# Feed-forward layers by seven block products instead of eight

## The chip, the cores and the metric

The kernel runs on one core of one Trainium2 chip. The metric is the device time of one execution in microseconds (us). The core has five engines, each with its own queue of instructions worked off in order: PE (TensorE, matrix products into PSUM), DVE (VectorE, elementwise), ACT (ScalarE, elementwise and functions), POOL (GpSimd, elementwise, reaches SBUF alone) and SP (which issues most DMAs). Semaphores make one engine wait for another.

## The reference

Two encoder layers are applied to 544 tokens (512 of a prompt, 32 of a sample) of 1024 features. Each layer is a feed-forward half step, a mixer (pooling, short convolution, differential attention with one input and one output projection) and a second feed-forward half step, each closed by a layer norm:

```python
def swiglu(x, w_in, w_out):
    gate, up = jnp.split(x @ w_in, 2, axis=-1)
    return (jax.nn.silu(gate) * up) @ w_out
...
    x = layer_norm(ALPHA * x + 0.5 * swiglu(x, w_ffn_in[0], w_ffn_out[0]), ln_g[0], ln_b[0])
    proj = x @ w_in
...
    x = layer_norm(ALPHA * x + mix, ln_g[1], ln_b[1])
    x = layer_norm(ALPHA * x + 0.5 * swiglu(x, w_ffn_in[1], w_ffn_out[1]), ln_g[2], ln_b[2])
```

The feed-forward width is 2816 (22 tiles of 128), so `w_in` is 1024 x 5632 and `w_out` 2816 x 1024. There are four such half steps, called FFNs here. Everything is float32.

## The kernel before

Activations lie feature by token: a tile is 128 features x 544 tokens, and all of x is eight tiles (`y[k]`). A product is taken on 128 features of output and half of the tokens (272) at a time, in one PSUM bank of six (`bank()`). To keep float32 accuracy each operand is split in a high and a low part that PE takes at one pass each: ACT copies the rounded high part (`whi`, `xh`, `hh`), DVE subtracts it from the original to give the low part (`wlo`, `xl`, `hl`). Each 128 x 128 block of weights then takes three matmuls on 272 columns: high by high, low by high (`mm_h`, L199), high by low (`mm_l`, L204).

Weights come from HBM by SP's queue into `raw` buffers, 512 KB at a time. `Weights.group` (L159 on ACT, L160 on DVE) splits 128 x 512 pieces into eight pairs of buffers. `W.get()` hands out the next tile and loads up to two tiles ahead.

`ffn` takes the 22 tiles of inner features in three parts, `FSPLIT = (8, 7, 7)`. In a part each inner tile needs a gate tile and an up tile: 8 blocks of weights x 3 matmuls x 2 halves x 2 = 96 matmuls. ACT takes the SiLU of the gate (L448), DVE multiplies by up (L449), and the result is split into `hh` and `hl` (L232, L233). Then eight output tiles are taken over the part's inner tiles and added to `y` (`resid`, L343 and L345). The last part ends in `out_phase`, where layer-norm sums run beside the products: DVE subtracts a shift from each finished tile, ACT squares it, POOL adds to two accumulators (L267 to L271, `acc1`, `acc2`). The last two output tiles (four in the very last layer norm) stand at the end by halves, so that the layer norm of the first half of the tokens runs beside the second half's products. `start` then takes the first two tiles of the next product while the layer norm is applied tile by tile.

The order on each engine is not that of the code: a scheduler that builds the program lays instructions out by readiness and priority, and semaphores keep what depends on what.

## Time and profile before

| | |
|---|---|
| time, median of 3 runs | 2105.5 us (2105.45 to 2107.89) |
| time of the profiled execution | 2106.86 us |
| span of the profiled execution, first to last instruction | 2104.7 us |
| PE busy | 2079.3 us, 99% of the span, 16286 matmuls |
| DVE busy | 1013.1 us, 48% |
| ACT busy | 771.6 us, 37% |
| POOL busy | 228.8 us, 11% |
| chain that ended last | PE 95%, DVE 2% |

The time is that of the whole execution; the span is what the trace shows of it and is 2.2 us shorter. Busy time counts a stretch once, also where two instructions of an engine overlap. A busy PE is not PE at its peak, since matmuls overlap in the records: how many matmuls start in a stretch says more than the mean length of one.

### The profile page before, as it was taken

How to read it: one execution, taken by the hardware profiler on the slowest of the kernel's cores; microseconds unless marked ns; L12 is line 12 of the kernel's file. 1: busy time of each engine (PE TensorE's matmuls, PEld its weight loads, DVE VectorE, ACT ScalarE, POOL GpSimd, SP SyncE). 2: the span in 40 equal slices, each digit the busy share in tenths (PEclk: the TensorE clock that was granted, in tenths of full speed). 3: DMA queues.
4: the chain of work that ended last, by engine and by line, in shares of the span. 5: the costliest groups of instructions: out<-in, count | busy, mean ns of one | idle time of the engine just before them, and what ended most of it. 6: DMA issues, size and time to landing. Idle time of an engine off the chain costs nothing.

```text
span 2104.7 us, 38545 instructions
## 1 busy us (share of the span) xinstructions
PE 2079.3 (99%) x16286; PEld 2042.2 (97%) x16286; DVE 1013.1 (48%) x1970; ACT 771.6 (37%) x1591; POOL 228.8 (11%) x216
## 2 busy tenths in 40 slices
PE   9999999999999999999999999999999999999997
PEld 9999999999999999999999999999999999999997
DVE  4333333776556333333653333347766553333337
ACT  5323223565435323223443232235653353222233
POOL 0000000511133000000420000006011320000003
PEclk9999999999999999999999999999999999999999
DMA  7322222132232222222232222222321222222221
GB/s 240 99 91 83 90 91 84 59 115 92 62 119 81 91 86 86 84 98 82 70 101 83 89 88 89 89 85 67 109 93 54 78 91 82 90 89 82 91 83 61
DMA packets 61749, 189.13 MB, mean 90 GB/s; under 512 B 8932, under 2 KB 13156, under 8 KB 61576
## 3 DMA queue, kind: packets, MB, share of 16 engines
q1 hardware_dynamic: 52592, 173.18, 25.9%
q10 hardware_dynamic: 8984, 13.49, 2.0%
q8 instruction: 128, 2.10, 0.4%
q14 instruction: 45, 0.37, 0.1%
HBM read 179.88 MB, written 8.34 MB: 89 GB/s over the span
## 4 chain that ended last, share of the span: by engine, by line
PE 95%; DVE 2%; POOL 1%; ACT 1%; issue 1%; DMA 0%; SPq 0%; POOLq 0%; ACTq 0%
PE b L199 59%; PE b L204 30%; PE b L629 1%; PE b L628 1%; PE o L644 1%; POOL xl L333 1%; PE b L609 0%; ACT ya L327 0%; DVE z L322 0%; PE b L716 0%; POOL rstd L302 0%; PE b L682 0%; DVE diag L308 0%; DVE acc L286 0%; PE b L311 0%
## 5 line engine op out<-in xcount | busy, mean ns | idle before, releaser
L199 PE MATMUL b<-xh,whi 128*128 128x272 f32 x3456 | 1000.0, 291 | 6.2 <-ACT xh L332 3.7
L199 PE MATMUL b<-xh,wlo 128*128 128x272 f32 x3456 | 993.5, 289 | 0.3 <-DVE wlo L160 0.3
L204 PE MATMUL b<-xl,whi 128*128 128x272 f32 x3456 | 978.2, 288 | 0.2
L160 DVE TENSOR_TENSOR wlo<-raw,whi 128x512 fp32r<-128x512 f32 (+1 forms) x656 | 469.7, 719 | 694.8 <-ACT whi L159 692.7
L159 ACT ACTIVATE whi<-raw 128x512 fp32r<-128x512 f32 (+1 forms) x656 | 403.3, 619 | 858.7 <-PE b L204 569.8
L199 PEld LDWEIGHTS b<-xh,whi 128*128 128x128 f32 x3456 | 651.7, 189 | 9.5 <-ACT xh L332 5.9
L199 PEld LDWEIGHTS b<-xh,wlo 128*128 128x128 f32 x3456 | 653.1, 189 | 1.5 <-DVE wlo L160 0.8
L204 PEld LDWEIGHTS b<-xl,whi 128*128 128x128 f32 x3456 | 644.6, 188 | 2.1 <-POOL xl L333 1.5
L199 PE MATMUL b<-hh,wlo 128*128 128x272 f32 x1408 | 406.2, 289 | 0.0
L199 PE MATMUL b<-hh,whi 128*128 128x272 f32 x1408 | 405.2, 288 | 0.0
L204 PE MATMUL b<-hl,whi 128*128 128x272 f32 x1408 | 404.6, 287 | 0.0
L199 PEld LDWEIGHTS b<-hh,wlo 128*128 128x128 f32 x1408 | 264.9, 188 | 0.2
L204 PEld LDWEIGHTS b<-hl,whi 128*128 128x128 f32 x1408 | 264.9, 188 | 0.2
L199 PEld LDWEIGHTS b<-hh,whi 128*128 128x128 f32 x1408 | 264.9, 188 | 0.0
L278 POOL TENSOR_TENSOR ya<-ya,shift 128x544 f32<-128x544 f32 x14 | 24.8, 1792 | 1412.9 <-DVE wlo L160 1386.4
L448 ACT ACTIVATE sg<-b 128x272 f32<-128x272 f32 x176 | 69.6, 397 | 213.1 <-PE b L204 213.0
L449 DVE SCALAR_TENSOR_TENSOR sg<-b,sg 128x272 f32<-128x272 f32 x176 | 77.6, 441 | 130.9 <-PE b L204 119.2
L343 DVE SCALAR_TENSOR_TENSOR ya<-ya,b 128x272 f32<-128x272 f32 x88 | 38.5, 438 | 88.7 <-PE b L204 87.8
L333 POOL TENSOR_TENSOR xl<-ya,xh 128x272 fp32r<-128x272 f32 x80 | 70.3, 901 | 30.8 <-ACT xh L332 25.1
L345 DVE TENSOR_TENSOR ya<-ya,b 128x272 f32<-128x272 f32 x108 | 46.7, 433 | 54.0 <-PE b L204 53.8
L232 ACT ACTIVATE hh<-sg 128x544 fp32r<-128x544 f32 (+1 forms) x100 | 59.1, 591 | 32.6 <-DVE sg L449 32.5
L233 DVE TENSOR_TENSOR hl<-sg,hh 128x544 fp32r<-128x544 f32 (+1 forms) x100 | 65.2, 652 | 7.2 <-ACT hh L232 7.1
(183 smaller groups left out, 1455.9 us busy)
## 6 DMA issues: line engine op xcount, KB each, us to landing
raw<-in_w SPq DMA_DIRECT2D x206, 512.0 KB, 3.5
raw<-in_w SPq DMA_DIRECT2D x64, 448.0 KB, 3.3
raw<-in_wi SPq DMA_DIRECT2D x40, 512.0 KB, 3.5
raw<-in_wo SPq DMA_DIRECT2D x16, 512.0 KB, 3.5
U<-scr ACTq DMA_DIRECT2D x8, 320.0 KB, 4.8
out_nkT<-k ACTq DMA_DIRECT2D x8, 272.0 KB, 2.1
out_nvT<-vT ACTq DMA_DIRECT2D x8, 272.0 KB, 2.1
out_yT<-ya SPq DMA_DIRECT2D x16, 136.0 KB, 1.8
```

The source lines that it names most:

```text
L159: S.activation(out=hi[:, :e], in_=raw[:, g:g + e], func=AF.Copy)
L160: V.tensor_tensor(out=lo[:, :e], in0=raw[:, g:g + e], in1=hi[:, :e].bitcast(F32), op=ALU.subtract)
L199: PE.matmul(acc[:, :HALF], v[:, cs], x[k][0][:, HS[h]], start=first and i == 0, stop=False)
L204: PE.matmul(acc[:, :HALF], w[k // 4][0][:, cs], x[k][1][:, HS[h]], start=False, stop=last)
L232: S.activation(out=hh[:, sl], in_=t[:, sl], func=AF.Copy)
L233: (eng or V).tensor_tensor(out=hl[:, sl], in0=t[:, sl], in1=hh[:, sl].bitcast(F32), op=ALU.subtract)
L278: POOL.tensor_tensor(out=c, in0=c, in1=self.s, op=ALU.subtract)
L333: POOL.tensor_tensor(out=xl[:, sl], in0=c, in1=xh[:, sl].bitcast(F32), op=ALU.subtract)
L343: V.scalar_tensor_tensor(out=c, in0=c, scalar=ALPHA, in1=a, op0=ALU.mult, op1=ALU.add)
L345: V.tensor_tensor(out=c, in0=c, in1=a, op=ALU.add)
L448: S.activation(out=sg[:, sl], in_=g[:, :HALF], func=AF.Silu)
L449: V.scalar_tensor_tensor(out=sg[:, sl], in0=u[:, :HALF], scalar=0.5, in1=sg[:, sl], op0=ALU.mult, op1=ALU.mult)
```

## The change

A product of a 2 x 2 arrangement of weight blocks with a 2 x 2 arrangement of activation blocks is eight block products; with sums of blocks formed beforehand, seven are enough. Here one dimension is the two halves of the tokens, one the two of a pair of input tiles (or input halves), and one the two outputs: gate and up of an inner tile, or two output tiles. `Weights.sums` forms four sums of weight blocks on DVE (L212 of the changed kernel) and splits seven groups (L177 on ACT, L178 on DVE) where four were split before. `Blocks.add` forms four sums of activations (L318 to L321) and splits two further tiles, `s56` and `s73`: on DVE for the x of each FFN, on POOL for pairs of inner tiles. `seven` takes the seven products (L343), called here by 0 to 6, into three banks in the order a, b, a, c, a, c, a; a bank is read after each product (`after`) and the next product of the same bank adds to what stands there, so it waits for that reading.

In each FFN the first two inner tiles (`NPLAIN`) are taken as before, the other 20 by `hidden`, with seven products of 12 matmuls. Output tiles are taken in pairs over parts of 4, 6, 6 and 6 inner tiles, by seven products of 6 or 9 matmuls, and added to `y` by `resid7` (L573, L575) after each product. The first part's outputs stand after the fifth inner tile, the second's after the eleventh, the third's after the seventeenth. In the last part the first pair and the last pair (the last two in the last layer norm) are taken as before. `W.get` loads one unit ahead; a unit is all seven groups. The tiles of the sums and of the layer norm lie in a pool `xb` that gives way to the mixer's pool. The weights are laid out by blocks on the host; their bytes are the same.

```diff
-FSPLIT = (8, 7, 7)
+FSPLIT = (4, 6, 6, 6)
+NPLAIN = 2
-RAW_BUFS = 2
+RAW_BUFS = 3
+XB = 23
...
+        def sums(self, b11, b12, b22, b21):
+            n = b11.shape[-1]
+            def add(a, b):
+                r = wp.tile([P, G], F32, tag="sum", name="sum", bufs=3)[:, :n]
+                V.tensor_tensor(out=r, in0=a, in1=b, op=ALU.add)
+                return r
+            g11, g21 = self.group(b11), self.group(b21)
+            r1 = add(b11, b12)
+            r2 = add(r1, b22)
+            g2, g1 = self.group(r2), self.group(r1)
+            g3 = self.group(add(b12, b22))
+            g22 = self.group(b22)
+            return g11, g21, g2, g1, g3, g22, self.group(add(r2, b21))
...
+        def add(self, e, o, eng, new):
+            h0, h1 = HS
+            t1, t2 = tmp("s56"), tmp("s73")
+            eng.tensor_tensor(out=t1[:, h0], in0=e[:, h1], in1=o[:, h1], op=ALU.subtract)
+            eng.tensor_tensor(out=t1[:, h1], in0=t1[:, h0], in1=e[:, h0], op=ALU.subtract)
+            eng.tensor_tensor(out=t2[:, h0], in0=e[:, h0], in1=e[:, h1], op=ALU.subtract)
+            eng.tensor_tensor(out=t2[:, h1], in0=o[:, h0], in1=t1[:, h1], op=ALU.add)
+            s = [f(n) for f, n in zip(new, ("s56", "s73"))]
+            split(t1, s[0])
+            split(t2, s[1])
+            self.sums.append(s)
+        def products(self):
+            e, o = ([self.plain[p[i]] for p in self.pairs] for i in range(2))
+            s56, s73 = ([s[i] for s in self.sums] for i in range(2))
+            for xs, h in ((e, 0), (o, 0), (s56, 1), (s56, 0), (s73, 0), (s73, 1), (o, 1)):
+                yield [tuple(v[:, HS[h]] for v in x) for x in xs]
+    def seven(ws, blocks, after):
+        banks = {}
+        for i, (w, xs, name) in enumerate(zip(ws, blocks.products(), "abacaca")):
+            opens = name not in banks
+            acc = banks.setdefault(name, bank() if opens else None)
+            for j, (xh, xl) in enumerate(xs):
+                cs = slice(j * P, (j + 1) * P)
+                for m, (v, x) in enumerate(((w[0], xh), (w[1], xh), (w[0], xl))):
+                    PE.matmul(acc[:, :HALF], v[:, cs], x, start=opens and j == 0 and m == 0,
+                              stop=j == len(xs) - 1 and m == 2, skip_group_check=True)
+            after[i](acc[:, :HALF])
...
+            if blocks and m:
+                seven(W.get(), blocks, resid7(m, alpha))
+                for i in range(2):
+                    done(m + i)
+                m += 2
+                continue
...
+    def resid7(m, alpha):
+        seen = set()
+        def step(i, h, op):
+            def f(acc):
+                c = y[m + i][:, HS[h]]
+                if alpha and (i, h) not in seen:
+                    V.scalar_tensor_tensor(out=c, in0=c, scalar=ALPHA, in1=acc, op0=ALU.mult, op1=op)
+                else:
+                    V.tensor_tensor(out=c, in0=c, in1=acc, op=op)
+                seen.add((i, h))
+            return f
+        add, sub = ALU.add, ALU.subtract
+        return [step(0, 0, add), step(0, 0, add), step(1, 0, sub), step(1, 1, add), step(1, 1, sub), step(1, 0, add),
+                step(0, 1, add)]
+    def hidden(ws, blocks):
+        sg = tmp("sg")
+        up = tp.tile([P, HALF], F32, tag="up", name="up", bufs=2)
+        h0, h1 = HS
+        copy = lambda out: lambda acc: S.activation(out=out, in_=acc, func=AF.Copy)
+        def times(u, sl):
+            V.scalar_tensor_tensor(out=sg[:, sl], in0=u, scalar=0.5, in1=sg[:, sl], op0=ALU.mult, op1=ALU.mult)
+        def c12(acc):
+            V.tensor_tensor(out=sg[:, h0], in0=acc, in1=sg[:, h0], op=ALU.subtract)
+            S.activation(out=sg, in_=sg, func=AF.Silu)
+            times(up, h0)
+        seven(ws, blocks, [
+            copy(up),
+            lambda acc: V.tensor_tensor(out=up, in0=acc, in1=up, op=ALU.add),
+            copy(sg[:, h0]),
+            copy(sg[:, h1]),
+            lambda acc: V.tensor_tensor(out=sg[:, h1], in0=sg[:, h1], in1=acc, op=ALU.subtract),
+            c12,
+            lambda acc: times(acc, h1),
+        ])
+        return sg
+    def is_last(l, f):
+        return l == DEPTH - 1 and f == 1
+    def plan(final):
+        ends = [sum(FSPLIT[:s + 1]) for s in range(len(FSPLIT))]
+        for i in range(NF):
+            yield 1, i, "p" if i < NPLAIN else "s"
+            if i in ends:
+                yield from ((2, ends.index(i), p, "s") for p in range(NK // 2))
+        tail = 2 if final else 1
+        for p in range(NK // 2):
+            yield 2, len(FSPLIT) - 1, p, "p" if p == 0 or p >= NK // 2 - tail else "s"
     def ffn(l, f, x, pre):
-        for s, n in enumerate(FSPLIT):
-            hs = []
-            for i in range(n):
-                if pre:
-                    ga, ua = pre
-                    pre = None
+        xb = Blocks(x, [(k, k + NK // 2) for k in range(NK // 2)])
+        for k in range(NK // 2):
+            xb.add(y[k], y[k + NK // 2], V, (new_b, new_b))
+        sgs, parts = [], []
+        for what, i, *more in plan(is_last(l, f)):
+            if what == 1:
+                if i < NPLAIN:
+                    ua, ga = pre if i == 0 else [run(mm2(w, x, range(NK))) for w in W.get()]
+                    sg = tmp("sg")
+                    for sl, g, u in zip(HS, ga, ua):
+                        S.activation(out=sg[:, sl], in_=g[:, :HALF], func=AF.Silu)
+                        V.scalar_tensor_tensor(out=sg[:, sl], in0=u[:, :HALF], scalar=0.5, in1=sg[:, sl],
+                                               op0=ALU.mult, op1=ALU.mult)
                 else:
-                    ga = run(mm2(W.get(), x, range(NK)))
-                    ua = run(mm2(W.get(), x, range(NK)))
-                sg = tmp("sg")
-                hx = new_x("h")
-                for sl, g, u in zip(HS, ga, ua):
-                    S.activation(out=sg[:, sl], in_=g[:, :HALF], func=AF.Silu)
-                    V.scalar_tensor_tensor(out=sg[:, sl], in0=u[:, :HALF], scalar=0.5, in1=sg[:, sl],
-                                           op0=ALU.mult, op1=ALU.mult)
-                    if i == n - 1:
-                        split(sg, hx, sl)
-                if i < n - 1:
-                    split(sg, hx)
-                hs.append(hx)
-            if s < len(FSPLIT) - 1:
-                for m in range(NK):
-                    acc = run(mm2(W.get(), hs, range(n)))
-                    for h in range(2):
-                        resid(m, acc[h], h, s == 0)
+                    sg = hidden(W.get(), xb)
+                sgs.append(sg)
+                if len(sgs) < 2:
+                    continue
+                n = len(parts[-1].plain) if parts else 0
+                if not parts or n == FSPLIT[len(parts) - 1]:
+                    parts.append(Blocks([], []))
+                    n = 0
+                part = parts[-1]
+                for t in sgs:
+                    part.plain.append(new_x("h"))
+                    split(t, part.plain[-1])
+                part.pairs.append((n, n + 1))
+                part.add(*sgs, POOL, {0: (new_b, new_b), 2: (new_b, new_x)}.get(n, (new_x, new_x)))
+                sgs = []
+            elif i < len(FSPLIT) - 1:
+                seven(W.get(), parts[i], resid7(2 * more[0], i == 0))
             else:
-                return out_phase(l, 2 * f, hs, range(n), False)
+                part = parts[i]
+                return out_phase(l, 2 * f, part.plain, range(FSPLIT[i]), False, part)
```

**DVE in the middle of a part.** In the kernel before, one inner tile's rows on DVE are four splits of weights (L160), two multiplications (L449) and a split of the result (L233):

```order
L449 SCALAR_TENSOR_TENSOR sg<-b,sg 128x272
L160 TENSOR_TENSOR wlo<-raw,whi 128x512
L449 SCALAR_TENSOR_TENSOR sg<-b,sg 128x272
L160 TENSOR_TENSOR wlo<-raw,whi 128x512
L233 TENSOR_TENSOR hl<-sg,hh 128x544
L160 TENSOR_TENSOR wlo<-raw,whi 128x512 x2
```

In the changed kernel twelve rows from about one inner tile's stretch read so (L604, L595, L601, L592 read PSUM or make the gated product; L212 sums weights, L178 splits them, L291 splits activations):

```order
L604 TENSOR_TENSOR sg<-sg,b 128x272
L595 TENSOR_TENSOR sg<-b,sg 128x272
L178 TENSOR_TENSOR wlo<-raw,whi 128x512
L178 TENSOR_TENSOR wlo<-sum,whi 128x512
L592 SCALAR_TENSOR_TENSOR sg<-up,sg 128x272
L592 SCALAR_TENSOR_TENSOR sg<-b,sg 128x272
L212 TENSOR_TENSOR sum<-raw 128x512
L178 TENSOR_TENSOR wlo<-raw,whi 128x512
L291 TENSOR_TENSOR hl<-sg,hh 128x544
L178 TENSOR_TENSOR wlo<-raw,whi 128x512
L601 TENSOR_TENSOR up<-b,up 128x272
L178 TENSOR_TENSOR wlo<-sum,whi 128x512 x2
```

Four weight rows for one inner tile have become eleven, and two that take results have become five.

**DVE where output tiles are added.** Before, an addition to `ya` (L345) stands once for each half of an output tile, with a split of weights between:

```order
L345 TENSOR_TENSOR ya<-ya,b 128x272
L160 TENSOR_TENSOR wlo<-raw,whi 128x512
L345 TENSOR_TENSOR ya<-ya,b 128x272
L160 TENSOR_TENSOR wlo<-raw,whi 128x384
L345 TENSOR_TENSOR ya<-ya,b 128x272
L160 TENSOR_TENSOR wlo<-raw,whi 128x512
L345 TENSOR_TENSOR ya<-ya,b 128x272
```

After, in the third part's first pair of output tiles, additions (L575) stand one for one with splits and sums:

```order
L592 SCALAR_TENSOR_TENSOR sg<-b,sg 128x272
L178 TENSOR_TENSOR wlo<-raw,whi 128x384
L575 TENSOR_TENSOR ya<-ya,b 128x272
L178 TENSOR_TENSOR wlo<-raw,whi 128x384
L575 TENSOR_TENSOR ya<-ya,b 128x272
L178 TENSOR_TENSOR wlo<-sum,whi 128x384
L575 TENSOR_TENSOR ya<-ya,b 128x272
L178 TENSOR_TENSOR wlo<-sum,whi 128x384
L212 TENSOR_TENSOR sum<-sum,raw 128x384
L575 TENSOR_TENSOR ya<-ya,b 128x272
L178 TENSOR_TENSOR wlo<-sum,whi 128x384
```

An addition now follows every nine matmuls, and more of DVE's rows stand between two additions.

**PE in the second pair of output tiles of the second part.** With buffer numbers; `b_2428` is bank b, `b_2417` bank a, `b_2449` bank c; the rows are the end of product 1, two thirds of product 3, and the beginning of product 2:

```order
L343 MATMUL b_2428<-hl_2109,whi_2272 128x272
L343 MATMUL b_2449<-s56h_1522,whi_2284 128x272
L343 MATMUL b_2449<-s56h_1522,wlo_2285 128x272
L343 MATMUL b_2449<-s56l_1523,whi_2284 128x272
L343 MATMUL b_2449<-s56h_1820,whi_2284 128x272
L343 MATMUL b_2449<-s56h_1820,wlo_2285 128x272
L343 MATMUL b_2449<-s56l_1821,whi_2284 128x272
L343 MATMUL b_2417<-s56h_1522,whi_2280 128x272
L343 MATMUL b_2417<-s56h_1522,wlo_2281 128x272
```

Product 3 has been moved ahead of product 2 there. Product 2 adds to bank a, which DVE reads after product 0; product 3 opens a bank of its own.

## Rows read from the trace of the kernel before

**Rows 1.** The page: span, then busy time, share and instructions of engines.

```profile
span 2104.7 us, 38545 instructions
...
PE 2079.3 (99%) x16286; PEld 2042.2 (97%) x16286; DVE 1013.1 (48%) x1970; ACT 771.6 (37%) x1591; POOL 228.8 (11%) x216
```

**Rows 2.** The page: shares of the chain that ended last, by engine.

```profile
PE 95%; DVE 2%; POOL 1%; ACT 1%; issue 1%; DMA 0%; SPq 0%; POOLq 0%; ACTq 0%
```

**Rows 3.** PE by line and shape: instructions, busy us, mean ns, idle before.

```profile
L199 PE MATMUL b<-xh,whi 128*128 128x272 f32 x3456 | 1000.0, 291 | 6.2 <-ACT xh L332 3.7 <-ACT msq L299 1.6 <-ACT whi L159 0.7
...
L199 PE MATMUL b<-hh,whi 128*128 128x272 f32 x1408 | 405.2, 288 | 0.0
```

**Rows 4.** Windows: busy us and count of PE, weight loads, DVE, ACT, POOL; granted clock.

```profile
240.00:330.00 90.00, 90.00 (x723) 90.00 (x722) 33.89 (x60) 24.72 (x44) 0.00 (x0) 1.00 0.29 92
405.00:418.00 13.00, 10.80 (x82) 9.72 (x81) 11.56 (x31) 10.36 (x26) 7.65 (x11) 1.00 0.00 0
545.65:555.88 10.23, 10.23 (x39) 9.04 (x40) 3.85 (x10) 3.00 (x9) 0.00 (x0) 0.50 0.09 33
```

**Rows 5.** DVE by line and shape: count, busy us, mean ns, idle before.

```profile
L160 DVE TENSOR_TENSOR wlo<-raw,whi 128x512 fp32r<-128x512 f32 x592 | 427.5, 726 | 677.1 <-ACT whi L159 675.0
...
L233 DVE TENSOR_TENSOR hl<-sg,hh 128x544 fp32r<-128x544 f32 x76 | 54.7, 720 | 1.2 <-ACT hh L232 1.1
L345 DVE TENSOR_TENSOR ya<-ya,b 128x272 f32<-128x272 f32 x108 | 46.7, 433 | 54.0 <-PE b L204 53.8
```

**Rows 6.** Timeline of DVE, 26 to 29 us: start, us, instruction, count merged.

```profile
26.31 0.72 DVE L233 TENSOR_TENSOR hl<-sg,hh 128x544 fp32r<-128x544 f32 x1 [0.39 <-ACT hh L232]
26.95 1.89 DVE L160 TENSOR_TENSOR wlo<-raw,whi 128x512 fp32r<-128x512 f32 x3
...
28.85 0.68 DVE L160 TENSOR_TENSOR wlo<-raw,whi 128x512 fp32r<-128x512 f32 x1
```

**Rows 7.** Timeline of DVE, 405 to 418 us.

```profile
409.81 1.47 DVE L322 TENSOR_TENSOR z<-ya,b 128x272 f32<-128x272 f32 x4
...
411.21 0.42 DVE L316 TENSOR_TENSOR ya<-ya,o 128x272 f32<-128x272 f32 x1
```

**Rows 8.** Timelines of DVE and of POOL, 384 to 400 us.

```profile
384.49 1.82 POOL L271 TENSOR_TENSOR acc<-acc,sq 128x544 f32<-128x544 f32 x1
...
385.00 0.42 DVE L345 TENSOR_TENSOR ya<-ya,b 128x272 f32<-128x272 f32 x1
385.35 1.37 DVE L160 TENSOR_TENSOR wlo<-raw,whi 128x384 fp32r<-128x384 f32 x1
...
388.82 1.37 POOL L271 TENSOR_TENSOR acc<-acc,sq 128x544 f32<-128x544 f32 x1
...
389.48 1.25 DVE L160 TENSOR_TENSOR wlo<-raw,whi 128x512 fp32r<-128x512 f32 x1 [1.77 <-ACT whi L159]
...
398.42 1.36 POOL L271 TENSOR_TENSOR acc<-acc,sq 128x544 f32<-128x544 f32 x1
...
398.49 1.60 DVE L285 TENSOR_TENSOR acc<-acc,ya 128x272 f32<-128x272 f32 x1 [0.22 <-POOL acc L270]
```

**Rows 9.** POOL by line and shape.

```profile
L333 POOL TENSOR_TENSOR xl<-ya,xh 128x272 fp32r<-128x272 f32 x80 | 70.3, 901 | 30.8 <-ACT xh L332 25.1 <-ACT msq L299 4.6
L271 POOL TENSOR_TENSOR acc<-acc,sq 128x544 f32<-128x544 f32 x28 | 41.7, 1490 | 0.0
```

**Rows 10.** ACT by line and shape.

```profile
L159 ACT ACTIVATE whi<-raw 128x512 fp32r<-128x512 f32 x592 | 369.9, 630 | 829.3 <-PE b L204 540.4 <-issue 265.2 <-DMA raw<-in_w 15.7
L448 ACT ACTIVATE sg<-b 128x272 f32<-128x272 f32 x176 | 69.6, 397 | 213.1 <-PE b L204 213.0
...
L232 ACT ACTIVATE hh<-sg 128x544 fp32r<-128x544 f32 x76 | 48.9, 643 | 0.8 <-DVE sg L449 0.7
```

More of the change, by code (lines that the diff above doesn't have):

```diff
@@ new lines, in load @@
+        def load(self):
+            kind, src, n, step = self.units[self.loaded]
+            self.loaded += 1
+            if kind == "t":
+                raw = self.fetch()
+                nc.sync.dma_start(out=raw[:, :n], in_=src)
+                out = Tile([self.group(raw[:, g:min(g + G, n)]) for g in range(0, n, G)])
+            elif kind == "p":
+                out = self.pair([self.group(b) for b in self.blocks(src, n)], step)
+            else:
+                out = self.sums(*self.blocks(src, n))
+            self.ready.append(out)
@@ L188, in ahead, with get @@
                 self.load()
[L190 removed]
+        def get(self, n=None):
+            if n is None:
+                n = 2 if self.units[self.used][0] == "t" else 1
             self.used += 1
@@ L193, in get, with two @@
             return self.ready.pop(0)
+        def two(self):
+            return self.get(0) if self.units[self.used][0] == "p" else [self.get(0), self.get(0)]
     def mm_h(acc, w, x, k, h, first):
-        cs = slice((k % 4) * P, (k % 4) * P + P)
-        for i, v in enumerate(w[k // 4]):
-            PE.matmul(acc[:, :HALF], v[:, cs], x[k][0][:, HS[h]], start=first and i == 0, stop=False)
+        for i, v in enumerate(w.at(k)):
+            PE.matmul(acc[:, :HALF], v, x[k][0][:, HS[h]], start=first and i == 0, stop=False)
     def mm_l(acc, w, x, k, h, last):
-        cs = slice((k % 4) * P, (k % 4) * P + P)
-        PE.matmul(acc[:, :HALF], w[k // 4][0][:, cs], x[k][1][:, HS[h]], start=False, stop=last)
+        PE.matmul(acc[:, :HALF], w.at(k)[0], x[k][1][:, HS[h]], start=False, stop=last)
     def mm(acc, w, x, ks, h):
@@ L352, in out_phase, with done @@
         first = NK - nb
-        for m in range(first):
-            acc = run(mm2(W.get(), x, ks))
-            for h in range(2):
-                resid(m, acc[h], h, alpha)
+        tail = []
+        def done(m):
             if m == 1:
@@ L363, in out_phase, with tiles @@
                     ln.before(i, alpha)
-        tail = [W.get() for _ in range(nb)]
+        def tiles():
+            ws = W.get()
+            return ws if isinstance(ws, list) else [ws]
+        m = 0
+        while m < first:
+            if blocks and m:
+                seven(W.get(), blocks, resid7(m, alpha))
+                for i in range(2):
+                    done(m + i)
+                m += 2
+                continue
+            for w in tiles():
+                acc = run(mm2(w, x, ks))
+                for h in range(2):
+                    resid(m, acc[h], h, alpha)
+                done(m)
+                m += 1
+        while len(tail) < nb:
+            tail += tiles()
         def tail_mm(i, h):
```

129 lines of the change are left out of this document (80 added, 49 removed).

## The prediction

> **What bounds the kernel now.** I read the page's busy times first: PE is busy for 2079.3 of 2104.7 us, DVE for less than half [rows 1]. The chain that ended last says the same, 95% PE [rows 2]. A busy PE could still be slow, so the windows come next: in the middle of an FFN 723 matmuls start in 90.00 us, 124.5 ns for each, at the full granted clock [rows 4]. PE has no idle time there to win; fewer matmuls is what can shorten it, as long as no other engine needs longer. DVE has room: 33.89 us busy of those 90.00 [rows 4]. The question is whether it still has room afterwards.
>
> **What is removed.** One FFN has 22 x 96 matmuls for gate and up and 22 x 48 for the outputs, 3168 in all, 394.4 us at 124.5 ns. (The trace has 3 x 1408 = 4224 on inner tiles, which is 4 x 1056, and 3 x 3456 on x, which holds 4 x 2112 and 1920 of the mixers' projections [rows 3].) Seven products instead of eight leave 84 of 96 in 20 inner tiles, 42 of 48 for each of four output pairs of the first part, 63 of 72 for each of eight pairs of the second and third and for two pairs of the last part (one in the last FFN). That is 354 fewer in three FFNs and 345 in the last, 1407, or 175 us; the order of the changed kernel has 13953 of these matmuls where there were 15360, so the change does what it says on PE. It is the ceiling: 1931 us, if nothing else took longer.
>
> **What DVE must do for it.** A price for DVE has to be what a row of instructions costs in a full queue, not the length of one. One 128 x 512 subtraction takes 726 ns in the mean [rows 5], but three in a row with a fourth's 0.68 us last took 1.89 us, so they start (1.89 - 0.68) / 2 = 0.605 us apart; the 544-column split just ahead of them started 0.64 us earlier [rows 6]. Four 272-column operations took 1.47 us, hence (1.47 - 0.42) / 3 = 0.35 us apart [rows 7]. On the line through these two, 384 columns take 0.47 and 256 columns 0.333 us. I price additions and subtractions of two tensors in SBUF, and those that read PSUM, alike, as the trace has both at 433 ns for 272 columns or near it.
>
> The Trainium skill (VectorE: DVE Perf Modes, Terms) speaks against this price: it says that DVE is flushed after every operation and the next can't issue until the pipe is empty. By that rule each would cost its whole length; the rows show starts closer than the lengths, so the trace doesn't agree. What it would give is the last rival below.
>
> POOL is the other part of the price. It now forms four sums of 272 columns for each of 11 pairs of inner tiles per FFN, at 0.90 us each [rows 9], 3.6 us a pair. DVE operations from SBUF stretch while POOL runs: a 384-column one took 1.37 us (0.8 too long) with 0.96 us of it beside a POOL instruction, a 512-column one 1.25 (0.56 too long) beside 0.71, a 272-column one 1.60 (1.17 too long) beside 1.29; the one that read PSUM kept its 0.42 us [rows 8]. Since not all of DVE's work is from SBUF and rows elsewhere stretch less (the mean of 726 ns is only 5% above a free one), I take 0.5 us lost for each us of POOL, bounds 0.2 and 0.9.
>
> **Stretch by stretch, one FFN.** The longer of PE's and DVE's need counts, since weights are made one unit ahead and a unit is some 10 us of slack.
>
> - Start: two plain inner tiles, 23.9 us of PE as before. DVE also has x's sums, 16 x 0.35 + 8 x 0.64 = 10.7 us, which can't begin before the layer norm has finished its tiles. Beside them stand four splits of the second tile (2.4), three splits and two sums for the first products by seven (3.0) and four products with the SiLU (1.4): 17.5 us against 96 + 24 matmuls, 14.9 us. PE waits 2.6 us; between 0 and 10.7.
> - Twenty inner tiles, ten pairs. PE: 168 matmuls, 20.9 us (23.9 before). DVE: 22 weight operations x 0.605 + 10 results x 0.35 + 4 splits x 0.64 = 19.4, and 1.8 for POOL: 21.2. So 212 us, 239 before. DVE is now the longer one by a hair.
> - Four output pairs of the first part. PE 42 matmuls, 5.2 us (6.0 before); DVE 11 x 0.333 + 7 x 0.35 = 6.1. So 24.4 us, 23.9 before: slower.
> - Eight output pairs of the second and third part. PE 63 matmuls, 7.84 us (8.96 before); DVE 11 x 0.47 + 7 x 0.35 = 7.6. So 62.7, 71.7 before.
> - Last part: two plain pairs, 17.9 us as before. In the two by seven DVE also subtracts the shift from two tiles (2 x 0.64) and POOL adds to its accumulators, four times 1.49 us [rows 9] at 0.5: 7.6 + 1.3 + 3.0 = 11.9 us each, 9.0 before. So 41.7, 35.8 before.
>
> Sum: 26.5 + 212 + 24.4 + 62.7 + 41.7 = 367.3 us against 394.4, 27.1 us less; the last FFN, with one such pair, 30.0 less. All four: 111 us.
>
> **Hand-overs.** Two engines with nearly the same need don't run without gaps. In the order after the change PE adds to a bank that was read only one product earlier, so it waits if that reading stands late in DVE's queue. The order eases it by letting product 3 go ahead of product 2, but not everywhere. Nothing in this trace has such a queue. I take half of one 0.605 us operation, 0.3 us, for each of the 135 units by seven: 40 us. The bounds are 0 (all found in other products) and 1.0 (a whole operation ahead and the reading's own 0.43 us, once a unit): 0 and 135 us.
>
> **Costs taken as nothing.** ACT: a pair of inner tiles needs 14 high parts, 6 copies, 2 SiLUs and 4 tile splits, at whole lengths [rows 10] 14 x 0.63 + 6 x 0.40 + 2 x 0.64 + 4 x 0.64 = 15.1 us of 21; uncovered it would be in the hand-overs. SP moves the same bytes with a third buffer, DMA engines 29% busy in the middle of an FFN [rows 4]. The mixer's pool waits for `xb` to be free; its bias tiles have three projections, 144 matmuls or 18 us, before they are read. The mixers and layer norms are otherwise untouched.
>
> 2106.9 (the profiled execution) - 111 + 40 = 2036 us; the median of the runs is 1.4 us lower than that execution, so **2035 us**.
>
> **Rivals.**
>
> - **DVE hides.** If POOL costs 0.2 us per us and hand-overs nothing, inner tiles fall to PE's 20.9 us and the two last pairs to 10.1: 3 x 4 us from the first, 13 from the second, 40 from the hand-overs, **1970 us**. For it: slack of a unit, PE's order adapted. Against: rows 8.
> - **PE waits at its banks.** One mechanism: readings of a bank stand behind splits and sums in DVE's queue, and the next product of that bank waits. It decides from 111 / 135 = 0.82 us a unit upwards; at 1.0 us the time is 2106 - 111 + 135, **2130 us**. For it: additions to `ya` now one for one with splits, each after only nine matmuls (1.1 us), where 0.43 us of reading and 0.47 of a split just fit. Against: every such wait lets DVE catch up.
> - **The clock.** In a mixer's stretch of short matmuls the granted clock was 0.50, the lower level of 1.2 GHz, for 10.23 us with 39 matmuls begun where the full clock gives 82 [rows 4]; at most 5.4 us each. With PE idle for 2.2 of 13 us it stayed at 1.00 [rows 4], so the short waits expected here don't lower it. If it fell once in each of 16 parts, 86 us: **2122 us**. The Trainium skill (TensorE: Matmul & The Clock Gate, Part 1) says that the low clock is what an idle PE falls back to, which is the same fear; its rule changes nothing in the sum.
> - **Whole lengths.** If each DVE operation cost its row's mean (0.726, 0.433, 0.72; 0.56 and 0.43 for the narrower ones), a pair of inner tiles would need 25.0 us (23.9 before), output pairs 9.2 and 7.8 (9.0 and 6.0), the last ones 13.6 (9.0), the start 5 more: 34 us more for each FFN, **2241 us**.
>
> **How the numbers follow.** Forecast 2035, its own range 1985 to 2085: 0.63. DVE hides 0.13; PE waits at its banks 0.16; the clock 0.03; whole lengths 0.03; 0.02 for no change. The range for 8 in 10 reaches down to 1965, below the second case, and up to 2125, into the third: 2 in 10 lie outside. A measurement of this kernel tells 0.2% (4 us) from no change. Faster are the first two and a little of the third, 0.78; same 0.03; slower 0.19.
>
> **What would show it.** Right: some 1407 fewer matmuls; DVE busy for over 80% of the span, about 95% in the middle of a part; PE's pitch still 124.5 ns where it runs, with gaps of under a us in front of the products that add to a bank, ended by DVE; output pairs of the first and last part longer than before, inner tiles some 10.7 us each instead of 11.95. Wrong: gaps of several us per unit, a granted clock of 0.50 in FFNs, DVE starts as far apart as their lengths, or inner tiles at 10.5 us with DVE idle.

## The result and the profile after

The changed kernel takes **2209.71 us** (median of 4 runs, 2205.36 to 2211.58) against 2106.15 (2105.45 to 2107.89) for the kernel before: 1.0487 times as long, 95% interval 1.0469 to 1.0506. The forecast was 2035 and the range ended at 2125: wrong in sign and outside the range.

The page of the changed kernel, span, busy times and chain by engine, beside [rows 1, 2]:

```profile
span 2209.2 us, 38708 instructions
...
PE 2002.9 (91%) x14879; PEld 1937.7 (88%) x14879; DVE 1835.0 (83%) x3620; ACT 1132.1 (51%) x2326; POOL 411.8 (19%) x392
...
PE 68%; DVE 15%; POOL 8%; ACT 5%; issue 4%; DMA 0%; POOLq 0%; SPq 0%; ACTq 0%; DVEq 0%
```

PE has its 1407 matmuls less, and DVE is at the forecast's "over 80%". But PE, 99% of the span before, now stands idle for 9%, and the chain leaves PE for a third of its length. The window in the middle of the first FFN (columns as in [rows 4]) began 723 matmuls before and begins 654 now:

```profile
240.00:330.00 90.00, 84.63 (x654) 83.48 (x654) 80.89 (x157) 47.34 (x90) 8.16 (x8) 0.98 0.30 94
```

Next, who lets PE wait. Waits of PE (us in total, times, longest), then the ones of ACT:

```profile
PE b L343 <- ACT up L589: 78.7, 33, 2.8
PE b L258 <- ACT sg L635: 34.4, 4, 12.6
PE o L404 <- DVE acc L397: 16.1, 6, 5.4
PE b L343 <- DVE ya L575: 15.6, 4, 4.5
PE b L343 <- ACT sg L589: 14.9, 8, 1.9
```

```profile
ACT s56h L290 <- POOL s L319: 107.1, 44, 2.9
```

The releaser that leads is neither DVE nor a sum but ACT's copies of banks (L589); ACT is busy for 51% of the span. ACT in turn waits 44 times, once for each of the 11 pairs of inner tiles in four FFNs, for POOL's sums of activations. One such place in timelines of PE (with the same wait two inner tiles later), ACT, POOL and DVE (start, length, idle before):

```profile
257.23 0.29 PE L343 MATMUL b<-xh,whi 128*128 128x272 f32 x1
260.30 0.40 PE L343 MATMUL b<-s56h,whi 128*128 128x272 f32 x1 [2.78 <-ACT up L589]
...
283.25 0.60 PE L343 MATMUL b<-s56h,whi 128*128 128x272 f32 x1 [2.54 <-ACT up L589]
```

```profile
254.38 0.66 ACT L290 ACTIVATE hh<-sg 128x544 fp32r<-128x544 f32 x1 [0.82 <-DVE sg L592]
254.94 0.61 ACT L177 ACTIVATE whi<-raw 128x512 fp32r<-128x512 f32 x1
257.94 0.66 ACT L290 ACTIVATE s56h<-s 128x544 fp32r<-128x544 f32 x1 [2.39 <-POOL s L319]
258.79 0.66 ACT L290 ACTIVATE s73h<-s 128x544 fp32r<-128x544 f32 x1 [0.19 <-POOL s L321]
259.35 0.61 ACT L177 ACTIVATE whi<-sum 128x512 fp32r<-128x512 f32 x1
259.87 0.38 ACT L589 ACTIVATE up<-b 128x272 f32<-128x272 f32 x1
```

```profile
254.46 1.07 POOL L318 TENSOR_TENSOR s<-sg 128x272 f32<-128x272 f32 x1 [19.38 <-DVE sg L592]
255.49 1.25 POOL L320 TENSOR_TENSOR s<-sg 128x272 f32<-128x272 f32 x1
256.70 1.21 POOL L319 TENSOR_TENSOR s<-s,sg 128x272 f32<-128x272 f32 x1
257.99 0.77 POOL L321 TENSOR_TENSOR s<-sg,s 128x272 f32<-128x272 f32 x1
```

```profile
249.67 0.68 DVE L212 TENSOR_TENSOR sum<-raw 128x512 f32<-128x512 f32 x1
250.27 0.43 DVE L604 TENSOR_TENSOR sg<-sg,b 128x272 f32<-128x272 f32 x1
250.62 0.69 DVE L178 TENSOR_TENSOR wlo<-raw,whi 128x512 fp32r<-128x512 f32 x1
...
255.07 1.04 DVE L291 TENSOR_TENSOR hl<-sg,hh 128x544 fp32r<-128x544 f32 x1 [0.19 <-ACT hh L290]
256.03 1.26 DVE L178 TENSOR_TENSOR wlo<-raw,whi 128x512 fp32r<-128x512 f32 x1
```

Read it from the end. PE's product 2 adds to bank a, so it needs that bank read; the reading is `up<-b` on ACT at 259.87. It stands fourth in ACT's queue behind `s56h`, which is at the head from 255.55 and waits until POOL has made three sums of a tile that DVE finished just before 254.38. PE stands still for 2.78 us, though what `s56h` prepares is needed only by output products that come later. The Trainium skill (PSUM — Partial Sum Buffer, Engine vs sequencer instructions) says that ACT's queue is strictly first in, first out; the trace agrees, 2.39 us of an idle ACT with a copy behind the head whose input was there (product 0's last matmul started at 254.09).

The second place is the start of an FFN. ACT from 698 us, the matmul that it lets wait, and three windows:

```profile
698.58 0.66 ACT L290 ACTIVATE s56h<-s 128x544 fp32r<-128x544 f32 x1 [2.77 <-DVE s L319]
...
702.53 0.66 ACT L290 ACTIVATE s56h<-s 128x544 fp32r<-128x544 f32 x1 [1.70 <-DVE s L319]
703.17 0.66 ACT L290 ACTIVATE s73h<-s 128x544 fp32r<-128x544 f32 x1
704.51 0.66 ACT L290 ACTIVATE s56h<-s 128x544 fp32r<-128x544 f32 x1 [0.68 <-DVE s L319]
705.18 1.28 ACT L635 ACT_TABLE_LOAD   x1
706.48 0.40 ACT L635 ACTIVATE sg<-b 128x272 f32<-128x272 f32 x1
```

```profile
706.93 0.59 PE L258 MATMUL b<-xh,whi 128*128 128x272 f32 x1 [7.48 <-ACT sg L635]
```

```profile
699.45:706.93 7.48, 0.00 (x1) 0.00 (x1) 7.48 (x16) 5.07 (x9) 0.00 (x0) 0.73 0.20 70
702.90:709.70 6.80, 2.77 (x12) 2.77 (x13) 6.09 (x13) 4.75 (x8) 0.00 (x0) 0.50 0.23 78
283.10:286.50 3.40, 3.25 (x14) 3.25 (x15) 1.54 (x4) 0.64 (x3) 0.00 (x0) 0.50 0.00 0
```

Here the splits of x's sums, which DVE makes one after the other, stand ahead of the SiLU (L635) that frees the first plain tile's banks; in the first FFN the same wait is 12.6 us. The granted clock is at 0.50, the level of 1.2 GHz, from 702.9, while PE is idle, until 709.7, and again for 3.4 us from 283.1, as a wait of 2.54 us at product 2 ends. The clock's records show 35 such stretches, 197.6 us in all; before there were 3, 28.9 us.

**Where the time is.** I split the span in two with the starts of L343's matmuls: "middle" is, in the four FFNs, from the first matmul of the 20 inner tiles by seven to the last one, with the outputs of three parts between them; "rest" is the span less that. For the kernel before, the middle is the forecast's 20 x 11.95 + 23.9 + 71.7 = 334.6 us for each FFN. The forecast's own sums stand below it: 4 x 299.1 + 128 x 0.3 in the middle, and in the rest 31 us for the starts and last parts and 7 x 0.3.

| us | middle, four FFNs | rest | span |
|---|---|---|---|
| before | 1338.4 | 766.3 | 2104.7 |
| forecast | 1234.8 | 799.4 | 2034.2 |
| changed kernel | 1337.7 | 871.5 | 2209.2 |

The middle misses by 103 us, the rest by 72. The same loss can be sorted by kind, from the distance between starts of matmuls: of the 280 us that came back against the 175 saved, 201 are in gaps of more than 300 ns between two starts (258 against 57 before), 49 in a low clock (54 against 5), 29 in shorter delays.

### The profile page after: what moved, and what is told of

It reads as the page before. It is cut to its first block, busy times and chain, and to the rows that moved or that the text cites. A ratio compares the mean times of both kernels' runs of the same rounds, so it can differ in the third digit from the quotient of the medians.

```text
span 2209.2 us, 38708 instructions
## 1 busy us (share of the span) xinstructions
PE 2002.9 (91%) x14879; PEld 1937.7 (88%) x14879; DVE 1835.0 (83%) x3620; ACT 1132.1 (51%) x2326; POOL 411.8 (19%) x392
## 4 chain that ended last, share of the span: by engine, by line
PE 68%; DVE 15%; POOL 8%; ACT 5%; issue 4%; DMA 0%; POOLq 0%; SPq 0%; ACTq 0%; DVEq 0%
PE b L343 43%; PE b L258 12%; PE b L262 6%; DVE wlo L178 5%; DVE sum L212 2%; ACT whi L177 2%; POOL s L319 2%; POOL s L320 2%; POOL s L318 2%; PE b L825 1%; PE b L824 1%; POOL s L321 1%; DVE sg L592 1%; PE o L840 1%; ACT s73h L290 1%
## 5 line engine op out<-in xcount | busy, mean ns | idle before, releaser
L177 ACT ACTIVATE whi<-raw 128x512 fp32r<-128x512 f32 (+2 forms) x585 | 338.1, 583 | 312.0 <-PE b L343 204.1
L177 ACT ACTIVATE whi<-sum 128x512 fp32r<-128x512 f32 (+2 forms) x540 | 301.1, 571 | 321.8 <-PE b L343 205.3
L178 DVE TENSOR_TENSOR wlo<-raw,whi 128x512 fp32r<-128x512 f32 (+2 forms) x585 | 407.0, 701 | 46.3 <-ACT whi L177 44.1
L178 DVE TENSOR_TENSOR wlo<-sum,whi 128x512 fp32r<-128x512 f32 (+2 forms) x540 | 329.3, 626 | 56.3 <-ACT whi L177 50.5
L343 PE MATMUL b<-s56h,whi 128*128 128x272 f32 x938 | 285.2, 305 | 97.0 <-ACT up L589 78.7
L258 PE MATMUL b<-xh,whi 128*128 128x272 f32 x896 | 272.9, 309 | 49.2 <-ACT sg L635 34.4
L343 PE MATMUL b<-s73h,whi 128*128 128x272 f32 x938 | 279.9, 299 | 15.3 <-ACT sg L589 14.9
L318 POOL TENSOR_TENSOR s<-sg 128x272 f32<-128x272 f32 x44 | 43.2, 982 | 1286.2 <-DVE sg L592 894.7
L343 PE MATMUL b<-s56h,wlo 128*128 128x272 f32 x938 | 280.0, 299 | 0.1
L343 PEld LDWEIGHTS b<-s56h,whi 128*128 128x128 f32 x938 | 185.0, 197 | 108.2 <-ACT up L589 86.6
L343 PE MATMUL b<-s56l,whi 128*128 128x272 f32 x938 | 278.9, 298 | 0.0
L343 PE MATMUL b<-xh,whi 128*128 128x272 f32 x960 | 278.0, 290 | 0.7 <-DVE sg L604 0.7
L343 PE MATMUL b<-xh,wlo 128*128 128x272 f32 x960 | 276.0, 288 | 0.2
L343 PE MATMUL b<-s73h,wlo 128*128 128x272 f32 x938 | 274.5, 293 | 0.0
L343 PE MATMUL b<-xl,whi 128*128 128x272 f32 x960 | 273.2, 287 | 0.0
L343 PE MATMUL b<-s73l,whi 128*128 128x272 f32 x938 | 271.6, 293 | 0.0
L258 PE MATMUL b<-xh,wlo 128*128 128x272 f32 x896 | 263.8, 298 | 0.1
L262 PE MATMUL b<-xl,whi 128*128 128x272 f32 x896 | 249.6, 298 | 1.4 <-POOL xl L445 1.4
L258 PEld LDWEIGHTS b<-xh,whi 128*128 128x128 f32 x896 | 177.7, 199 | 55.4 <-ACT sg L635 35.3
L343 PEld LDWEIGHTS b<-s73h,whi 128*128 128x128 f32 x938 | 182.3, 195 | 23.0 <-ACT sg L589 19.3
L343 PEld LDWEIGHTS b<-s56h,wlo 128*128 128x128 f32 x938 | 186.1, 198 | 1.0 <-DVE wlo L178 1.0
L343 PEld LDWEIGHTS b<-s56l,whi 128*128 128x128 f32 x938 | 186.3, 199 | 0.0
```

The costliest lines, as they stand in the source:

```text
L177: S.activation(out=hi[:, :n], in_=raw, func=AF.Copy)
L178: V.tensor_tensor(out=lo[:, :n], in0=raw, in1=hi[:, :n].bitcast(F32), op=ALU.subtract)
L258: PE.matmul(acc[:, :HALF], v, x[k][0][:, HS[h]], start=first and i == 0, stop=False)
L262: PE.matmul(acc[:, :HALF], w.at(k)[0], x[k][1][:, HS[h]], start=False, stop=last)
L318: eng.tensor_tensor(out=t1[:, h0], in0=e[:, h1], in1=o[:, h1], op=ALU.subtract)
L343: PE.matmul(acc[:, :HALF], v[:, cs], x, start=opens and j == 0 and m == 0, stop=j == len(xs) - 1 and m == 2, skip_group_check=True)
```

## The experiments

Theory A: the order on ACT. Splits that wait for sums of activations stand ahead of readings of banks that PE waits for; the low clock follows from PE's waits. Theory B: DVE's amount of work, stretched by POOL, is what everything waits for. The times below that come from a single run (1 to 4, 7, 11 and 12) stand beside 2107.1 to 2108.6 us of the kernel before on the same chip. "Middle" and "rest" are as in the table.

**1. Pair sums on DVE.**

```diff
-                part.add(*sgs, POOL, ...)
+                part.add(*sgs, V, ...)
```

> The four sums of each pair of inner tiles are formed on DVE instead of POOL. Theory A (order on ACT: the split of s56 stands ahead of the copy of bank a and waits for POOL's sums; PE waits for that copy): the sums are ready some 3 us sooner, the 85 us of PE's waits at product 2 nearly go, and with them some low clock: about 2100 us. Theory B (DVE is at its limit among the inner tiles, POOL's sums stretch its operations): DVE gets 4 x 0.35 = 1.4 us a pair more and loses about 3.8 us of stretching, 44 times 2.4 us less: about 2105 us. This run alone does not tell them apart; slower than 2180 would speak against both.

Measured 2084.77 us, span 2082.9: middle **1208.7** (302.1 in each FFN), rest 874.2. One edit makes the middle 129 us shorter and puts it below the forecast's 1234.8. DVE has more to do and makes the sums sooner. Of PE's waits, the copies of banks (L589) that led before are gone, and these two lead now:

```profile
PE b L258 <- ACT sg L635: 34.5, 4, 12.6
PE b L343 <- DVE ya L575: 20.2, 12, 4.5
```

Both theories asked for some 2100 us, so alone it doesn't tell A from the part of B that blames POOL.

**2. The same sums on POOL, later in the order** (behind product 3 of the next inner tile).

```diff
+        def c3(acc):
+            copy(sg[:, h1])(acc)
+            while mid:
+                mid.pop()()
...
-                part.add(*sgs, POOL, ...)
+                mid.append(lambda part=part, sgs=sgs, new=new: part.add(*sgs, POOL, new))
...
```

> The sums stay on POOL, but they and their splits are written after product 3 of the following inner tile, so that on ACT they stand behind the copy of bank a. Theory A: the waits at product 2 go, 85 us and part of the low clock: 2090 to 2125 us. Theory B: DVE has the same work and the same stretching, so the time stays within 20 us of 2209.

Measured 2127.92 us, middle 1255.4, rest 870.7. The same instructions on the same engines, 82 us less: 3 us above A's range and far from B's. PE's waits at product 2 are gone; these two lead:

```profile
PE b L258 <- ACT sg L640: 34.4, 4, 12.6
PE b L343 <- ACT sg L589: 27.1, 20, 1.9
```

POOL's stretching is still there (POOL 438.1 us busy) and is not what cost the 82 us: in the middle, DVE's instructions beside POOL are together 74 us longer than the median of their like without POOL, where it was 55 in the changed kernel. The edit moves POOL's and DVE's rows along with ACT's; that the order on ACT is the one that counts is read from the waits, and no run moves ACT's rows alone.

**3. x's sums later** (behind the first plain tile's SiLU and product).

```diff
-        for k in range(NK // 2):
-            xb.add(y[k], y[k + NK // 2], V, (new_b, new_b))
...
+                    if i == 0:
+                        for k in range(NK // 2):
+                            xb.add(y[k], y[k + NK // 2], V, (new_b, new_b))
```

> The sums of x at the start of each FFN are written after the first plain inner tile's results are taken, so that ACT's SiLU of that tile no longer stands behind their splits. Theory A: about 10 us of PE's wait and some low clock go in each of four FFNs: 2150 to 2170 us. Theory B: DVE has the same work before the first product by seven, so the wait moves there: within 15 us of 2209.

Measured 2176.2 us: middle 1343.6, rest **830.8**, 41 less than in the changed kernel. A's second place is shown; the gain in all, 34 us, is 6 us short of A's range.

**4. Four weight additions per unit left out** (the second summand is used as the sum).

```diff
-                V.tensor_tensor(out=r, in0=a, in1=b, op=ALU.add)
-                return r
+                return b
```

> The four additions of weight blocks of each unit are left out (one block is split in the sum's place), so the products are not the reference's; PE, ACT, SP and POOL have the same work, DVE 4 x 0.605 us less for each inner tile. Theory B: inner tiles fall from 12.9 us towards PE's 10.5: 2010 to 2060 us. Theory A: DVE was not what PE waited for; ACT's waits for POOL stay: 2170 to 2205 us.

Measured 2222.42 us, middle 1357.8, rest 862.8. The window of [rows 4] and two waits (two lines of the code are gone, so L341 is what was L343):

```profile
240.00:330.00 90.00, 84.85 (x640) 84.30 (x639) 64.11 (x119) 46.58 (x89) 7.66 (x8) 0.94 0.29 89
```

```profile
PE b L341 <- ACT up L587: 103.4, 40, 2.9
```

```profile
ACT s56h L288 <- POOL s L317: 112.2, 44, 2.7
```

DVE has lost a fifth of its work (64 us busy of 90 instead of 81), and PE waits more at product 2, not less: 40 times instead of 33. B falls for the changed kernel. A's range was missed too, by 17 us: gaps of more than 300 ns are 17 us less in all, but the clock was low for 287.8 us instead of 197.6, which cost 35 us more. Why it fell more often here is open.

**5. Edits 1 and 3 together.**

> The pair sums go to VectorE (as in the run with the sums on VectorE, 2084.8 us) and the activation sums at the start of a layer are written behind the first plain tile's SiLU and product (33.5 us less than the changed kernel when done alone). Theory A, the order on ScalarE's in-order queue: the two waits stand at different places, so the gains add: 2084.8 - 33.5 = about 2051 us, between 2040 and 2065, and the plain-tile gaps fall from 63 us to about 28. Theory B, VectorE at its limit: VectorE has the same work as in the run with the sums on it, so the time stays at 2085 within 10 us.

Measured 2067.01 us (2061.62 to 2067.09), 0.9801 of the time before, interval 0.9786 to 0.9816: between the theories, nearer to A. Rest 835.2, 39 less than with edit 1 alone, as A says; but the middle grew from 1208.7 to 1229.5. Part of x's sums now stand behind the first product by seven, where DVE has little room: in the first FFN eight of the 16, and its middle grew from 302.1 to 309.4 us.

**6. With 5, the last part's pairs by eight, without its sums.**

```diff
-            if blocks and m:
+            if blocks and m and False:
...
-        tail = 2 if final else 1
...
-            yield 2, len(FSPLIT) - 1, p, "p" if p == 0 or p >= NK // 2 - tail else "s"
+            yield 2, len(FSPLIT) - 1, p, "p"
...
+                if len(parts) < len(FSPLIT):
+                    part.add(*sgs, V, ...)
```

> As the run with both changes, but every pair of output tiles of the last part is done by eight products, with no sums. TensorE gets 63 matmuls of 124.5 ns more, 7.8 us. Theory A: the waits at product 2 of the last part (about 17 us) and some of those at the transposes that follow the last sums (25 us) go with the sums that caused them: 10 to 30 us less, net 0 to 20 us below the run with both. Theory B, VectorE's work in the last part sets the end of a layer: less work there by some 20 us in four layers, and nearly the same time, so the two differ only if the time gets longer: by the 7.8 us of TensorE if neither wait was caused by the sums.

Measured **2025.94 us** (2023.0 to 2029.24), 0.9613, interval 0.9597 to 0.9629: 41 us less than 5, twice what A gave at most. Rest 795.5, 40 less; middle 1230.8. Part of it is the clock, low for 71.0 us in all where it was 118.1, worth 8 us in the distances of matmuls. Both theories ask for this direction, so it sizes the last part and doesn't decide.

**7. With 1, 90 matmuls that nobody reads between the first and second plain tile.**

```diff
+                    if i == 1:
+                        fill = side()
+                        for _ in range(90):
+                            PE.matmul(fill[:, :HALF], ones128, x[0][0][:, HS[0]], start=True, stop=True)
```

> As the run with the sums on VectorE (2084.8 us), with 90 matmuls whose result nobody reads written between the first and the second plain tile of each layer, where TensorE stands idle for about 12.6 us and its clock is low behind that. If the low clock there follows from the idle time: the clock stays at full speed in the stretches at the layers' starts, and each layer gains up to half of its low stretch of 7 to 10 us, 4 x 3 to 5 = 12 to 20 us, less what the extra matmuls cost where they outlast the wait (90 x 124.5 ns = 11.2 us against 12.6). So 2065 to 2080 us. If the low clock has another cause: 2080 to 2095 us, with the same low stretches.

Measured 2084.57 us, as without them and inside the range expected of another cause. The start of the second FFN, in run 1 and here:

```profile
660.00:690.00 30.00, 22.09 (x150) 21.50 (x151) 25.09 (x48) 16.31 (x30) 2.66 (x3) 0.83 0.16 53
```

```profile
660.00:690.00 30.00, 29.84 (x238) 29.62 (x239) 25.75 (x49) 17.18 (x32) 3.00 (x3) 1.00 0.17 54
```

Yet with PE kept busy the clock stays at its upper level there, so it was the idle time that lowered it, as the first theory says. It gains nothing: the 88 further matmuls are the fillers themselves. Low stretches fell from 153.5 to 106.7 us in all, worth 7 us of matmul distance, and the fillers cost 8 us more than the waits they filled (360 x 0.1245 = 45 against 37).

**8. With 5, all outputs by eight, gate and up by seven.** The last part as in 6, and:

```diff
-                yield from ((2, ends.index(i), p, "s") for p in range(NK // 2))
+                yield from ((2, ends.index(i), p, "p") for p in range(NK // 2))
...
-                part.add(*sgs, V, ...)
...
-                seven(W.get(), parts[i], resid7(2 * more[0], i == 0))
+                for m, wt in enumerate(W.get(), 2 * more[0]):
+                    acc = run(mm2(wt, parts[i].plain, range(FSPLIT[i])))
+                    for h in range(2):
+                        resid(m, acc[h], h, i == 0)
```

> As the run with both changes, but all output products are done by eight (no pair sums, no output combinations), gate and up still by seven. TensorE gets 447 matmuls of 124.5 ns more than the run with both, 55.7 us. Theory A (what is left of the waits is small once the splits don't stand ahead of the banks): the time rises by most of it, less the 35 to 45 us of waits left at product 2 and at the end of a layer: 2060 to 2105 us. Theory B (VectorE is the limit, and the output products by seven are what overloads it): the time falls below the run with both, 2010 to 2045 us.

Measured 2037.59 us (2033.22 to 2041.01), 0.9673, interval 0.9657 to 0.9689: 29 us *less* than 5 with 55.7 us more of matmuls. That is B's range: behind the order, the work that outputs by seven bring is the limit. This edit takes work from ACT and hand-overs from PE too; run 12 takes work from DVE alone. The time is 12 us more than run 6's, which has only the last part by eight: the middle's outputs by seven are worth 12 of their 384 x 0.1245 = 48 us, those of the last part less than nothing.

**9. Edits 2 and 3 together: order alone.**

> The changed kernel with the same instructions on the same engines (pair sums on GpSimd), and only the order in which two things are written: the pair sums and their splits behind product 3 of the next inner tile (2127.9 us alone), and the activation sums at a layer's start behind the first plain tile's SiLU and product (2176.2 us alone). Theory A, the order on ScalarE's queue: the two gains add, 2209.7 - 81.8 - 33.5 = 2094 us; with the 16 us that were lost when the same second edit was put on the run with the sums on VectorE, 2110. So 2090 to 2115 us. Theory B, VectorE's amount of work keeps the rest: what is moved comes back as another wait, 2120 to 2135 us.

Measured 2122.37 us (2121.15 to 2123.42), 1.0067, interval 1.005 to 1.0084: B's range. Rest 834.5, 36 less than in run 2; middle 1284.9, 30 more. What is left in PE's waits, and ACT's for POOL:

```profile
PE b L343 <- ACT sg L589: 32.7, 23, 2.7
...
PE b L343 <- DVE ya L575: 15.6, 4, 4.5
PE b L343 <- DVE sg L609: 14.7, 20, 2.2
```

```profile
ACT s56h L290 <- POOL s L319: 56.2, 27, 4.2
```

Order alone gives back 87 of the 104 us lost against the kernel before. Part of ACT's wait for POOL's sums is left, 56 us of 107, and PE now waits at other readings; POOL's slow sums in the middle do cost, 1284.9 against 1229.5 with the sums on DVE.

**10. With 6, the pair sums later in the order.** As in 2, on DVE:

```diff
-                    part.add(*sgs, V, ...)
+                    mid.append(lambda part=part, sgs=sgs, new=new: part.add(*sgs, V, new))
```

> The run with the last part by eight products (2025.9 us), with its pair sums, on VectorE, written behind product 3 of the next inner tile. What is left there of waits in the inner tiles is about 5 us at product 2, 3 at product 6, and 18 us at the output products of the finished parts, whose sums VectorE brings late. Theory A, order still counts: 5 to 20 us less, 2006 to 2021 us. Theory B, what is left is VectorE's amount of work, which this does not change: within 6 us of 2026, or some us more, since the sums come later and the output products of a finished part wait longer for them.

Measured 2026.62 us (2020.14 to 2030.76), 0.9609, interval 0.9587 to 0.9631: no difference from 6, as B says. With the sums on DVE order has nothing more to give at that place.

**11. The changed kernel with the last part's pairs by eight.**

> The changed kernel (2209.7 us) with nothing but the last part's pairs of output tiles by eight products, and no sums for that part. TensorE gets 63 matmuls, 7.8 us. If the waits in the last part and at the layer norm behind it come from those sums: product 2's 16.8 us and half of the 22.7 us at the statistics' matmuls go, and some 10 us of low clock: 2209.7 + 7.8 - 17 - 11 - 10 = 2180 us, between 2165 and 2190. The same edit was worth 41 us behind the two others. If the waits at a layer's end only come from work that was late before it: 2205 to 2220 us.

Measured 2148.58 us, 61 less and more than expected: rest 832.1 (39 less), and 23 less in the middle (1314.7), since two of the last part's three pair sums, with their waits (2.0 and 2.8 us in the first FFN, at 341.7 and 365.9), stand between inner tiles; the third comes after the last.

**12. Edits 1 and 4 together.**

> The run with the pair sums on VectorE (2084.8 us), with the four additions of weight blocks per unit left out (the second summand stands in for each sum, so the output is not the reference's); leaving them out of the changed kernel itself made it no faster (2222.4 us). In the run with the sums on VectorE the stretch of 20 inner tiles and three parts' outputs takes 302.1 us in each layer, where TensorE's own need is 20 x 10.46 + 4 x 5.23 + 8 x 7.84 = 292.8. Theory A, first the order on ScalarE's queue, and behind it VectorE's amount of work: with the order out of the way the same edit now counts, 293 to 296 us for the stretch, 2045 to 2062 us in all. Rival: what is left of the stretch are hand-overs that less work on VectorE doesn't shorten: 300 us or more, 2072 to 2086 us.

Measured 2039.64 us, 5 less than A's range; middle 1186.4 (296.6 in each FFN, 0.6 above A's), 22 less than in run 1, and the rest 23 less. The window of [rows 4] for run 1, for this one and for run 6:

```profile
240.00:330.00 90.00, 90.00 (x709) 89.08 (x709) 88.78 (x182) 51.95 (x98) 0.00 (x0) 1.00 0.34 103
```

```profile
240.00:330.00 90.00, 90.00 (x718) 89.89 (x717) 74.71 (x145) 53.66 (x101) 0.00 (x0) 1.00 0.32 98
```

```profile
240.00:330.00 90.00, 90.00 (x705) 88.70 (x704) 87.79 (x178) 50.76 (x96) 0.00 (x0) 1.00 0.33 100
```

The edit that made the changed kernel 13 us slower makes this one 45 faster. In run 1 DVE is busy for 88.78 of 90 us; with less to do PE's pitch goes from 127 ns to 125. First A, and behind it B: the same edit shows both.

## Why the prediction was wrong

**The removal** was right: 1407 matmuls less, at 124.5 ns 175 us.

**DVE's price in the middle** was right. Sums start 0.60 us before the next operation and 272-column ones 0.35 (249.67, 250.27 and 250.62 above; forecast 0.605 and 0.35), closer together than their lengths, so "whole lengths" fell. The price of POOL was right too: the split at 256.03 took 1.26 us instead of 0.69 wholly beside POOL, 0.45 us for each us of POOL, and over the whole middle DVE's instructions were 55 us longer for 136 us beside POOL, 0.40 (forecast 0.5). The Trainium skill (SBUF — State Buffer, Who interferes with whom) says that a VectorE instruction with two inputs in SBUF contends with a GpSimd one that reads SBUF; the row agrees. With the wait for POOL out of the way the middle took 302.1 us an FFN (run 1). There the sums cost DVE 4 x 0.35 = 1.4 us a pair instead of 1.8, so by the forecast's prices a pair takes PE's 20.9 us, and the sum without hand-overs is 209 + 24.4 + 62.7 = 296.1.

**The step that failed** is "ACT: ... 15.1 us of 21; uncovered it would be in the hand-overs", with the hand-overs taken as half of one DVE operation, 0.3 us for each unit by seven. I counted ACT's work and not its order. A queue that is busy for half its time was the bound, because a split at its head waited for POOL's sums with PE's readings behind it. Measured over the middle's 128 units, (1337.7 - 1196.4) / 128 = 1.1 us a unit, above the bound of 1.0; with the sums on DVE (1208.7 - 4 x 296.1) / 128 = 0.2, close to the 0.3. So the size of a hand-over on DVE held, and what was missing is ACT's wait for POOL. POOL made it longer: its four sums have a mean of 0.98, 1.17, 1.23 and 0.87 us, 4.2 us a pair and not 3.6.

```profile
L319 POOL TENSOR_TENSOR s<-s,sg 128x272 f32<-128x272 f32 x44 | 54.1, 1229 | 0.0
L320 POOL TENSOR_TENSOR s<-sg 128x272 f32<-128x272 f32 x44 | 51.3, 1166 | 0.0
L318 POOL TENSOR_TENSOR s<-sg 128x272 f32<-128x272 f32 x44 | 43.2, 982 | 1286.2 <-DVE sg L592 894.7 <-ACT whi L177 272.5 <-DVE sg L636 119.0
...
L321 POOL TENSOR_TENSOR s<-sg,s 128x272 f32<-128x272 f32 x44 | 38.3, 870 | 3.4
```

**The start** was given 2.6 us of waiting an FFN, bound 10.7. The bound is DVE's work; again it was ACT's queue that handed it to PE, 34.4 us in four waits, 8.6 in the mean and 12.6 in the first FFN, above the bound. Moving the sums took 41 us from the rest (run 3), 10 for each FFN, but DVE has to do them elsewhere: where DVE was at its limit, 21 (run 5 against 1) or 30 us (run 9 against 2) came back in the middle, and where PE still waited for other things only 6 (run 3).

**The last part** was forecast 5.9 us longer in three FFNs and 2.9 in the last, some 21 in all. Taking it back saved 39 us of the rest (run 11; 40 in run 6 against 5), though it costs 7.8 us of matmuls: measured, the loss is nearly twice the forecast's, the low clock included.

**The rivals.** "PE waits at its banks" had the right mechanism and the wrong queue: the readings stood behind splits in ACT's queue, the releaser was POOL, and it came with a price above the one I took as the end. "The clock" was dismissed since short waits had not lowered it in one window [rows 4]. Here a wait of 2.54 us came with a low clock (283.25) and one of 2.78 us did not (260.30, after which the clock's records show 1.00 to 264). It cost 49 us more than before. Mostly it follows the waits: it shrank in runs that took them away (197.6 us of low clock in the changed kernel, 153.5 in run 1, 71.0 in run 6), and keeping PE busy removed it in the window shown of run 7; but in run 4 it grew while gaps shrank.

What stays open: which of the waits lower the clock; how the last part's 39 us divide between DVE's work there and the waits at the layer norm's sums; and what holds the rest at 795.5 us in run 6, with both places mended, where 766.3 and the 10 forecast for the starts make 777.

## What to carry to other kernels

An engine that is busy half the time is not free: look at what stands in its queue ahead of each reading that the bound engine waits for, and when that thing's own inputs come. Work that is needed late, with inputs from a slow engine, belongs behind such readings, or on the engine that makes it soonest, even if that one is the busier (run 1: 125 us). After an order is mended the next bound shows, so price each part of a saving alone: seven products pay for gate and up and for outputs in the middle, and not for the last part of a layer (2025.9 us, 3.9% below the kernel before).

## What was not expected of the hardware

The contention of VectorE and GpSimd runs both ways. VectorE's split of 512 columns took 1.26 us beside GpSimd (256.03) instead of 0.69, and GpSimd's sums of 272 columns took 1.25 us beside two of VectorE's splits (255.49) and 0.77 with VectorE all but idle (257.99). The two seem to take turns rather than to share. In the changed kernel, 25 splits of 512 columns started while one of POOL's sums ran, and most of them ended 0.55 us after that sum's end; 139 of POOL's sums started while a VectorE operation on two tensors in SBUF ran, and most ended 0.62 to 0.64 us after its end. The rows at 254 to 258 us show the chain: ends at 255.53 (POOL), 256.11 (DVE), 256.74 (POOL), 257.29 (DVE) and 257.91 (POOL). So the later instruction loses about what is left of the earlier one.
